# A 256 MB quadrant swap by DMA on one core: every half row on the sync queue, and SBUF copies of 2 to 6 KB issued from the scalar queue

## The chip, the cores and the metric

The kernel runs on one core of one Trainium2 chip. The metric is device time in microseconds (us). Two runs of the kernel before took 810.55 and 813.21 us, a median of 811.88 us. One further execution was taken with the hardware profiler; its own time is the span of 812.4 us, from the first to the last instruction.

A core has 16 DMA engines. They serve DMA queues that are filled by the sequencers of other engines: here SP (SyncE, the "sync queue") and ACT (ScalarE, the "scalar queue"). In the profile the two queues are q1 and q10. A DMA is cut into packets; here a packet is one contiguous run of bytes.

## The reference

```python
x = np.random.randn(8192, 8192).astype(np.float32)
return np.fft.ifftshift(x)
```

For even sizes this swaps the quadrants: `out[r, c] = x[(r + 4096) % 8192, (c + 4096) % 8192]`. Nothing is computed. 268.44 MB are read from HBM and 268.44 MB are written to HBM, in half rows of 4096 float32, which is 16 KB each.

## The kernel before, in words

Each DMA goes straight from HBM to HBM. It moves 256 half rows (4 MB): 16 half rows for each of the 16 DMA engines. The function `copy` (L26 to L32) writes the pattern as `[[C, 16], [step*C, 16], [1, 4096]]`. The first dimension is the DMA engine, so with `step = 16` engine e takes the rows e, e+16, e+32 and so on, and at any moment the 16 engines work on neighbouring rows.

There are 64 such DMAs. The loop at L36 to L39 issues them in pairs: SP copies the left half of 256 rows of the output (L38), ACT the right half of 256 rows that lie 512 rows away within the same group of 1024 rows (L39). So each queue has 32 DMAs.

What holds the issuing back is bookkeeping of the tile framework. It gives each DMA one of eight completion semaphores in turn, and a DMA waits until the one that had this semaphore before it is complete. The turn is the order that the framework's scheduler gives to the program, and not that of the text. In the kernel before SP and ACT alternate in that order, so each queue has four DMAs in flight, eight in all. No DMA depends on another one's data.

Of the kernel before, what the change touches and what calls it, by code (L numbers as in the profile page):

```python
# [1 line left out]

# [4 lines left out]


ENGINES = 16


@with_exitstack
def kernel(
    ctx: ExitStack,
    tc: tile.TileContext,
    x: bass.AP,
    out: bass.AP,
):
    nc = tc.nc
    R, C = x.shape  # L20
    hr = R // 2
    hc = C // 2
    per = 16
    rows = ENGINES * per

    def copy(queue, row, h, step):  # L26

        dims = [[C, ENGINES], [step * C, per], [1, hc]]
        queue.dma_start(
            out=bass.AP(out.tensor, out.offset + row * C + h, dims),  # L30
            in_=bass.AP(x.tensor, x.offset + (row + hr) % R * C + hc - h, dims),
        )  # L32

    for first in range(0, R, 4 * rows):  # L36
        for n in range(4):
            copy(nc.sync, first + n * rows, 0, ENGINES)  # L38
            copy(nc.scalar, first + (n + 2) % 4 * rows, hc, ENGINES)  # L39


# [1 line left out]
_INS = ['x']  # L43
_OUTS = [((8192, 8192), 'float32')]


def kernel(**inputs):
    import numpy as _np
    import concourse.bacc as _bacc
    import concourse.tile as _tile  # L50
    from concourse import mybir as _mybir
    from concourse.bass_utils import run_bass_kernel_spmd as _run

    nc = _bacc.Bacc("TRN2", target_bir_lowering=False, num_devices=1)  # L54
    arrays, args = {}, []
    for name in _INS:
        a = _np.ascontiguousarray(inputs[name])
        if a.dtype.kind in "iu":
            a = a.astype(_np.int64)
        arrays[f"in_{name}_dram"] = a  # L60
        args.append(nc.dram_tensor(f"in_{name}_dram", a.shape, _mybir.dt.from_np(a.dtype), kind="ExternalInput").ap())
    for i, (shape, dtype) in enumerate(_OUTS):
        dt = _mybir.dt.from_np(_np.dtype(dtype))
        args.append(nc.dram_tensor(f"out_{i}_dram", shape, dt, kind="ExternalOutput").ap())
    with _tile.TileContext(nc) as tc:
        kernel(tc, *args)
    r = _run(nc, [arrays], core_ids=[0])
    got = tuple(r.results[0][f"out_{i}_dram"] for i in range(len(_OUTS)))
    return got[0]
```

## Time and profile before

| what | value | where it stands |
|---|---|---|
| median of two runs | 811.88 us (810.55 and 813.21) | the times |
| profiled execution, own time = span | 812.4 us | the profile's page |
| HBM read and written | 268.44 MB and 268.44 MB, 661 GB/s together | the page, part 3 |
| DMAs on SP's and on ACT's queue | 32 and 32, of 4096 KB each | the page, part 6 |
| packets in all | 17408, of which 1024 under 512 B (16 for each of the 64 DMAs) | the page, part 2 |
| time from issue to landing, median | 101.0 us | the page, part 6 |

The compute engines do nothing here, apart from four small memsets of POOL at the start. So the chain of waits on the page has nothing to say, and the profile is read from its DMA rows: the busy share of the 16 DMA engines and the GB/s that they moved, in 40 slices of the span or in stretches that one chooses. "GB/s" counts each byte once, though it is read from HBM and written to HBM: 330 GB/s moved is 660 GB/s at the HBM.

### The profile page before, as it was taken

How to read it: one execution, taken by the hardware profiler on the slowest of the kernel's cores; microseconds unless marked ns; L12 is line 12 of the kernel's file. 1: busy time of each engine (PE TensorE's matmuls, PEld its weight loads, DVE VectorE, ACT ScalarE, POOL GpSimd, SP SyncE). 2: the span in 40 equal slices, each digit the busy share in tenths (PEclk: the TensorE clock that was granted, in tenths of full speed). 3: DMA queues.
4: the chain of work that ended last, by engine and by line, in shares of the span. 5: the costliest groups of instructions: out<-in, count | busy, mean ns of one | idle time of the engine just before them, and what ended most of it. 6: DMA issues, size and time to landing. Idle time of an engine off the chain costs nothing. (4 is left out here: it accounts for less than half of the span.)

```text
span 812.4 us, 109 instructions
## 1 busy us (share of the span) xinstructions
POOL 0.2 (0%) x4
## 2 busy tenths in 40 slices
POOL 0000000000000000000000000000000000000000
DMA  9999999999999999999999999999999999999998
GB/s 307 331 331 336 335 331 331 335 325 337 334 332 336 331 333 332 334 339 332 332 334 331 329 331 334 332 328 333 330 334 335 334 328 333 332 331 330 338 331 280
DMA packets 17408, 268.44 MB, mean 330 GB/s; under 512 B 1024, under 2 KB 1024, under 8 KB 1024
## 3 DMA queue, kind: packets, MB, share of 16 engines
q1 hardware_dynamic: 8704, 134.22, 49.7%
q10 hardware_dynamic: 8704, 134.22, 49.5%
HBM read 268.44 MB, written 268.44 MB: 661 GB/s over the span
## 5 line engine op out<-in xcount | busy, mean ns | idle before, releaser
L54 POOL MEMSET const-bfloat16-1.0<- 128x1 bf16 x1 | 0.1, 101 | 0.0
L54 POOL MEMSET const-uint8-127<- 128x1 uint8 x1 | 0.1, 101 | 0.0
L54 POOL MEMSET const-float32-0.0<- 128x1 f32 x1 | 0.1, 98 | 0.2 <-issue 0.2
L54 POOL MEMSET const-float32-1.0<- 128x1 f32 x1 | 0.1, 98 | 0.0
## 6 DMA issues: line engine op xcount, KB each, us to landing
out_dram<-in_x_dram SPq DMA_DIRECT2D x32, 4096.0 KB, 101.0
out_dram<-in_x_dram ACTq DMA_DIRECT2D x32, 4096.0 KB, 101.0
```

What stands on the lines that cost most here:

```text
L54: nc = _bacc.Bacc("TRN2", target_bir_lowering=False, num_devices=1)
```

## The change

All 64 copies of half rows are issued from SP (`nc.sync`, L42). Per 1024 rows of the output (an "eighth"), the order is now four DMAs of the left half and then four of the right half.

After each copy, except in the last eighth, ACT issues a `pace(n)` (L47 to L50): a DMA from one SBUF tile, `idle`, to a tile of a pool with six buffers, `into`. It moves `[128, 2, n]` float32 out of tiles of `[128, 2, 2064]`, so it consists of 256 runs of 4n bytes, 16 runs for each DMA engine. That is one run of SBUF bytes for each half row that the engine copies. `n` is 512, 768, 1024, 1280, 1536, 1024, 768 in the first seven eighths: runs of 2, 3, 4, 5, 6, 4 and 3 KB. There are 56 such DMAs, which move 56.6 MB. What they write is never read. VectorE fills `idle` with zeros once (L35), and the first `pace` waits for that.

In the sixth and seventh eighth `apart` is 16 and `by` is 1: engine e takes 16 rows that follow each other, and the 16 engines work 16 rows (512 KB) apart.

```diff
+    still = ctx.enter_context(tc.tile_pool(name="still", bufs=1))
+    paced = ctx.enter_context(tc.tile_pool(name="paced", bufs=6))
+    idle = still.tile([128, 2, longest + 16], f32)
+    nc.vector.memset(idle[:], 0.0)
-    def copy(queue, row, h, step):
+    def copy(row, h, apart, by):
-        dims = [[C, ENGINES], [step * C, per], [1, hc]]
-        queue.dma_start(
+        dims = [[apart * C, ENGINES], [by * C, per], [1, hc]]
...
+        nc.sync.dma_start(
...
+    def pace(n):
+        into = paced.tile([128, 2, longest + 16], f32, name="into")
+        nc.scalar.dma_start(out=into[:, :, :n], in_=idle[:, :, :n])
-    for first in range(0, R, 4 * rows):
-        for n in range(4):
-            copy(nc.sync, first + n * rows, 0, ENGINES)
-            copy(nc.scalar, first + (n + 2) % 4 * rows, hc, ENGINES)
+    part = 1024
+    for n, (piece, apart) in enumerate((
+        (512, 1), (768, 1), (1024, 1), (1280, 1), (1536, 1),
+        (1024, per), (768, per), (0, 1),
+    )):
+        for h in (0, hc):
+            for row in range(n * part, (n + 1) * part, rows):
+                copy(row, h, apart, ENGINES if apart == 1 else 1)
+                if piece:
+                    pace(piece)
```

The built program can be read before it runs. Call the copies C1 to C64 and the SBUF copies P1 to P56, each in the order of its queue. The scheduler put them, and so handed out the eight semaphores, in this order: C1, P1 to P34, C2, P35 to P56, C3 to C64. The waits that came of it are these (the letter after "waits" is the DMA that must be complete):

```
SP queue                       ACT queue
C1   waits for nothing         P1        waits for the memset of idle
C2   waits P27                 P2 to P6  wait for nothing
C3   waits P49                 P7        waits P1
C4   waits P50                 P8        waits P2 and C1
C5   waits P51                 P9 to P41 wait for the P six before (P9: P3)
...                            P42       waits P36 and C2
C10  waits P56                 P43 to P56 wait for the P six before
C11  waits C3
C12  waits C4, and so on to C64, which waits C56
```

## The prediction

> **What bounds the kernel now.** I read the page's DMA rows first, because no compute engine does anything.
>
> ```profile
> span 812.4 us, 109 instructions
> ...
> DMA  9999999999999999999999999999999999999998
> GB/s 307 331 331 336 335 331 331 335 325 337 334 332 336 331 333 332 334 339 332 332 334 331 329 331 334 332 328 333 330 334 335 334 328 333 332 331 330 338 331 280
> ...
> q1 hardware_dynamic: 8704, 134.22, 49.7%
> q10 hardware_dynamic: 8704, 134.22, 49.5%
> HBM read 268.44 MB, written 268.44 MB: 661 GB/s over the span
> ```
>
> All 16 DMA engines are busy in every slice, and the rate is flat at 332 GB/s. The two queues' packets fill 99.2% of the engines' time, so there is no gap to fill. Busy is not the same as at full speed, though. 99.2% of 16 x 812.4 us over 16384 data packets is 787 ns for a packet of 16 KB. In the trace's packet records the commonest duration is 611 ns (4,842 of the 16,384 packets), hardly any is shorter, and the others spread up to some 1,400 ns. I take 611 ns (26.8 GB/s, or 429 GB/s for 16 engines) as what an engine can do and the other 176 ns as waiting for the HBM, where all 16 engines read and write at once.
>
> Then I cut the span into stretches (us, length; then POOL, clock, DMA share, GB/s moved):
>
> ```profile
> 2.00:3.00 1.00, 0.00 (x0) 1.00 1.05 262
> 3.00:4.00 1.00, 0.00 (x0) 1.00 1.01 410
> 4.00:5.00 1.00, 0.00 (x0) 1.00 1.00 377
> 5.00:6.00 1.00, 0.00 (x0) 1.00 1.11 426
> 6.00:8.00 2.00, 0.00 (x0) 1.00 0.98 344
> 8.00:10.00 2.00, 0.00 (x0) 1.00 1.01 344
> 10.00:20.00 10.00, 0.00 (x0) 1.00 0.99 328
> ...
> 100.00:400.00 300.00, 0.00 (x0) 1.00 1.00 333
> ...
> 806.00:808.00 2.00, 0.00 (x0) 1.00 0.96 328
> ```
>
> From 3 to 6 us the kernel moved 404 GB/s, more than ever after. Up to 5 us only SP's queue had packets and the 16 engines ran in step. By 10 us both queues were at work, the engines had drifted apart, and the rate was that of the rest. The last row matters as well: in 806 to 808 us SP's queue had nearly run out (85% of the bytes were on ACT's queue by the packet records), the engines were out of step, and the rate was 328 GB/s.
>
> Last, the DMA queue's own waits, with what the sequencers waited for:
>
> ```profile
> SPq L29 <- DMA out_dram<-in_x_dram: 689.4, 28, 25.3
> SPq L65 <- DMA out_dram<-in_x_dram: 102.2, 2, 79.5
> ```
>
> The sequencers wait for landings for nearly all of the span, 25 us at most (two DMAs of 12.6 us). These waits cost nothing while eight DMAs are in flight. They cost all they last when what is awaited is not a copy of half rows, and that is where the change goes.
>
> **The change part by part.** The sum is made against the profiled execution, 812.4 us, 0.5 us above the median of the runs. At 332 GB/s a copy of 4.194 MB costs 12.63 us; 64 of them are 808.5 us, and 3.9 us are start and end (the first packet starts at 2.2 us).
>
> *The order.* The text reads as if each SBUF copy ran beside its half rows. The built program's waits say otherwise: C2 waits for P27, C3 for P49, C4 to C10 for P50 to P56. So the first 49 SBUF copies run with only C1 and C2 beside them, and the other 62 copies come after, with hardly any pacing. Where the HBM had work all the time, it now idles while SBUF copies to SBUF.
>
> *The first stretch, up to the landing of P49.* P1 to P48 are eight each of 512, 768, 1024, 1280, 1536 and 1024 columns, and P49 one of 768; a column is 1024 bytes (128 x 2 x 4). That is 51.1 MB, 3.19 MB for each engine. The trace of before has no SBUF copy. The floor is the 611 ns row, 26.8 GB/s: 119 us. The upper bound is the mean HBM packet, 787 ns for 16 KB: 154 us. I take the floor, because these packets don't touch the HBM, which is what makes the 787; I add 9 ns a packet, which is what a 4-byte semaphore packet takes in the records, for 49 x 16 packets: 7 us, together 126 us. Six SBUF copies are in flight, 7 us of work at the shortest length (1.2 us each), against 0.6 us to issue one and 1.4 us from issue to first packet, so latency doesn't show. The packets of C1 and C2 run on the same engines: 2 x 16 packets at the 656 to 689 ns of the first rounds, 21 us (ends 20 and 25). With the start at 2.2 us the stretch ends at 149 us, between 141 and 181. The memset of 4128 columns by VectorE isn't in the trace (the nearest row is POOL's 0.1 us for one column); C1's packets fill the engines until 12 us, so up to there it costs nothing, and beyond that it would cost what it takes longer. P8 waits for C1 and P42 for C2, which are done before.
>
> *Handing over.* C3 waits for P49, and from that landing to its first packet lie 0.6 us of issue and 1.4 us: 2 us, in which P50 to P55 go on.
>
> *P50 to P56.* 5.5 MB, 12.8 us of engine time at the floor, beside C3 to C10. Nothing of it shows if the half rows' packets only shorten their wait for the HBM (176 ns each, against 115 ns for a 3 KB run); all of it shows if not. I take the middle, 6 us.
>
> *The 62 other copies.* From C11 on each waits for the one eight before it, so eight are in flight as before, all on one queue. The row nearest to one queue with engines out of step is the 328 GB/s of 806 to 808 us; the row with one queue and engines in step is 404 GB/s. Here the engines come out of a mixture of SBUF and HBM packets, and nothing puts them in step again, so I take the steady 332: 62 x 12.63 = 783 us. The fast end is 62 x 10.4 = 644 us. For the slow end I take 3% more, the spread of the slices: 807 us. That left and right halves are 1024 rows in turn, and that C41 to C56 put the engines 512 KB apart, has no row of its own and stands within these ends.
>
> The sum is 149 + 2 + 6 + 783 + 2 (the end) = **942 us**, 130 more than before. Against 812.4: 147 us up to P49, 2 + 6 after it, less C1 and C2 that are done by then (25 us).
>
> Two places of the Trainium skill bear on the 62 copies. The Trainium skill's page HBM Reference, section Specifications (TRN2), gives about 716 GB/s for the HBM of a pair of cores; by it one core moves at most 358 GB/s from HBM to HBM, the 62 copies take at least 726 us and the whole at least 885. The trace does not agree in its first microseconds: 404 GB/s moved is 808 at the HBM, though for 3 us only. The Trainium skill's page DMA: Bandwidth & Descriptors, section Latency and other measured facts, has copies at a row pitch of 512 KiB at 207 GB/s where 214 was full rate; if that held for the 512 KB between engines in C41 to C56, it would add an estimated 7 us (16 x 12.63 x 0.034), and the sum would be 949. No trace here shows it.
>
> **The rivals.**
>
> *One queue keeps the engines in step* (ends on the other side). If it is the second queue that pulls the engines out of step, the 62 copies could go at the start's 404 GB/s: 149 + 2 + 6 + 644 + 2 = 803 us, no slower than before. For it speaks that the rate fell as ACT's packets came in. Against it speak 806 to 808 us, with one queue and 328 GB/s, and that packets of up to 1,188 ns come already in the fourth round of SP's packets. It decides from 11.6 us a copy (361 GB/s), which gives 878, below the lower end of the sum; it makes the change no slower by 2% (828 us) only from 10.8 us a copy (389 GB/s).
>
> *The pacing runs as the text reads*, one SBUF run for each half row, should the waits bind less than I read them. Then either the HBM stays the limit and the SBUF runs hide in its 176 ns (812 us and some more where runs are 5 and 6 KB: 611 + 191 and 611 + 229 ns are over 787, which is 15 and 53 ns on 2048 packets an eighth, over 16 engines 2 and 7 us, so 821), or the engines' time adds up (56.6 MB at 429 GB/s, 132 us, so 944). Against it stand the waits of the built program, which are counts that must be reached.
>
> *SBUF copies or one queue are slower than any row here.* At half the floor rate (13.4 GB/s an engine) P1 to P49 take 238 us and the whole is 1054. Nothing in the trace speaks for it but that it has no such row.
>
> **How the numbers follow.** I give the forecast 0.68, the rival with engines in step 0.15 (of it 0.02 faster and 0.04 within 2%), pacing as the text reads 0.05 (0.02 within 2%, the rest slower), and slower rows 0.12. The forecast's own range is 141 + 2 + 0 + 783 + 2 = 928 to 181 + 2 + 13 + 783 + 2 = 981. The range for 8 in 10 reaches down to 875, which takes in the weaker half of the first rival (one queue a little faster), and up to 985. Faster by over 2%: 0.02. Within 2%, about what a measurement of this kernel can tell from no change: 0.06. Slower by over 2%: 0.92.
>
> **What would show it.** In the profile after, the HBM moves its 661 GB/s only from some 150 us on. Before that ACT's queue carries 51 MB, the rate moved is near 429 GB/s, and only two of SP's copies have landed. SP's second issue comes near 70 us (P1 to P27 are 22.8 MB, 53 us, plus C1 and the start), its third near 149 us, and the longest wait of its queue is about 80 us. Afterwards the rate is 332 GB/s with packets of about 787 ns. I am wrong if the third copy is issued much before 140 us, if the last 600 us run far from 332 GB/s, or if SBUF packets of 2 to 6 KB take much more than 80 to 240 ns.

## The result, and the profile after

The changed kernel took 943.71 us (median of two runs, 940.75 and 946.67) against 811.88 us: 1.163 times as long, with a 95% interval of 1.153 to 1.173. Its profiled execution has a span of 938.6 us.

The DMA rows of the page after:

```profile
span 938.6 us, 168 instructions
...
DMA  9999999999999999999999999999999999999998
GB/s 322 409 416 402 423 417 404 377 376 334 333 330 330 335 331 337 335 326 334 338 335 330 336 336 334 332 337 335 334 337 336 333 333 338 333 332 332 332 336 294
...
q1 hardware_dynamic: 17408, 268.44, 84.6%
q10 hardware_dynamic: 15232, 56.63, 15.0%
HBM read 268.44 MB, written 268.44 MB: 572 GB/s over the span
```

The DMA engines are as busy as before, in every slice. They also move more: 346 GB/s on average. Neither line shows the loss. The last line does: the HBM went from 661 to 572 GB/s, which is the same bytes over a longer span. The row of GB/s says where. In the second to seventh slice (each is 23.5 us) the engines move above 400 GB/s, which HBM traffic never did for long before, and from the tenth slice up to the last but one it is at 326 to 338, as before.

The waits of SP's queue (us in total, times, longest):

```profile
SPq L42 <- DMA into<-idle: 205.5, 9, 78.2
SPq L87 <- DMA out_dram<-in_x_dram: 68.1, 4, 31.2
```

Nine times SP's queue waited not for a copy of half rows but for an SBUF copy, 205.5 us in all and 78.2 us the longest. Those are the waits of C2 to C10. The order of issue shows two of them (start, length, then engine, line and how many without a gap in between):

```profile
59.73 21.62 ACTq L50 DMA_DIRECT2D into<-idle  x6
71.55 0.59 SPq L42 DMA_DIRECT2D out_dram<-in_x_dram  x1
```

```profile
140.83 12.07 ACTq L50 DMA_DIRECT2D into<-idle  x6
150.34 9.96 SPq L42 DMA_DIRECT2D out_dram<-in_x_dram  x4
```

SP's second copy was issued at 71.55 us and the third at 150.34 us, half a microsecond after P49 had landed (149.8 us by the sixteenth of its semaphore packets). Cut at these points (us, length; VectorE, POOL, clock, DMA share, GB/s moved):

```profile
2.00:16.00 14.00, 3.16 (x1) 0.00 (x0) 1.00 0.98 324
16.00:71.00 55.00, 0.00 (x0) 0.00 (x0) 1.00 1.03 412
71.00:92.00 21.00, 0.00 (x0) 0.00 (x0) 1.00 1.01 399
92.00:150.00 58.00, 0.00 (x0) 0.00 (x0) 1.00 1.02 419
150.00:161.00 11.00, 0.00 (x0) 0.00 (x0) 1.00 1.03 394
161.00:212.00 51.00, 0.00 (x0) 0.00 (x0) 1.00 1.00 378
212.00:930.00 718.00, 0.00 (x0) 0.00 (x0) 1.00 1.00 334
```

In the second and the fourth stretch, 113 us together, the packet records hold not one packet of 16 KB: all of it is SBUF to SBUF, and the HBM idles. The first stretch holds C1, the third C2. From 212 us on it is the kernel before on one queue, at 334 GB/s.

The HBM idles longer than these two stretches, because the packets of C2 and C3 start late: C2's first one at 76.68 us, 5.1 us after its issue, and C3's at 155.50 us, 5.2 us after. By the packet records no half row is under way from 16.1 to 76.7 us and from 90.5 to 155.5 us, which is 125.6 us together. The span is 126.2 us longer than that of the kernel before, so this is all but the whole loss.

### The profile page after: what moved, and what is told of

Read it like the earlier page. It is cut to its first block, busy times and chain, and to the rows that moved or that the text cites. A ratio compares the mean times of both kernels' runs of the same rounds, so it can differ in the third digit from the quotient of the medians.

```text
span 938.6 us, 168 instructions
## 1 busy us (share of the span) xinstructions
DVE 3.5 (0%) x1; POOL 0.2 (0%) x4
## 5 line engine op out<-in xcount | busy, mean ns | idle before, releaser
L35 DVE MEMSET idle<- 128x4128 f32 x1 | 3.5, 3498 | 1.7 <-PEq L76 1.7
```

The source lines that it names most:

```text
L35: nc.vector.memset(idle[:], 0.0)
```

## The experiments

The theory, called the order theory below: the 132 us (943.71 less 811.88) were lost because the built order puts 49 SBUF copies ahead of 62 copies of half rows, so the HBM idles while they run. It has a rival with the same sum for this kernel: SBUF bytes take the DMA engines' time wherever they stand, and 56.6 MB at 410 to 429 GB/s are 132 to 138 us. A second rival puts the loss on the one queue and the row patterns. The first three runs tell these apart. The last three measure what an SBUF run costs. The first three kernels share runs of the kernel before with a median of 810.97 us. The last three were timed later, together with runs of the kernel before that took 823.41 us; why those took 1.5% more is not known. Each ratio is to the runs of its own group.

**The copies alone, on one queue.**

```diff
-    nc.vector.memset(idle[:], 0.0)
+    nc.vector.memset(idle[:, :, :16], 0.0)
...
                 copy(row, h, apart, ENGINES if apart == 1 else 1)
-                if piece:
-                    pace(piece)
```

> The changed kernel without its 56 SBUF copies (so it leaves out only work that the output does not need): 64 copies of half rows on SP's queue in the same order and with the same row patterns, eight in flight. Order theory (the loss is the time in which SBUF copies run with at most two copies of half rows beside them): 64 x 12.63 us and 4 us at the ends, 812 us, within 1% of before. Rival, one queue or the row patterns cost or gain something by themselves: the time differs from 812 by what they do, above 828 if they cost; if one queue kept the engines in step (404 GB/s) about 670.

Measured: 814.85 us against 810.97, a ratio of 1.005 (1.002 to 1.008). The page of that run:

```profile
GB/s 302 327 321 334 328 324 332 331 322 335 321 339 335 334 337 337 333 327 335 340 330 334 332 332 328 329 335 339 331 330 331 334 337 334 340 335 331 331 330 294
...
q1 hardware_dynamic: 17408, 268.44, 99.2%
HBM read 268.44 MB, written 268.44 MB: 660 GB/s over the span
```

The one queue and the patterns cost half a per cent, 4 of the 132 us. One queue does not hold the 404 GB/s of the start either: the rate is flat at 332 from the second slice on. The Trainium skill's page DMA: Bandwidth & Descriptors, section Issuing engines are not separate DMA queues, says that a second issuing engine only saves the time of issuing; this run agrees, with 1.005 for one queue in place of two. The eighths with the engines 512 KB apart stand out in nothing: 100.9 and 100.0 us against 100.4 to 101.9 for the second to fifth. The forecast took 3% for them from the Trainium skill's page DMA: Bandwidth & Descriptors, section Latency and other measured facts, where the pitch of 512 KiB lies between the rows of partitions. Between these two patterns the 3% did not appear. In the other eighths, though, the rows of one engine lie 512 KB apart, so no run here shows a copy without that pitch.

**The same 120 DMAs, in the order of the text.** Each DMA gets an edge of issue order to the one before it, which orders the scheduler and adds no wait:

```diff
+    def behind(one, other):
...
+            tc.add_manual_dep(
+                one.ins,
+                other.ins.name,
+                mybir.DependencyInfo(
+                    mybir.DependencyClass.NoSync, mybir.DependencyReason.DATA
+                ),
+                reason="order",
+            )
+        return one
...
-                copy(row, h, apart, ENGINES if apart == 1 else 1)
+                last = behind(copy(row, h, apart, ENGINES if apart == 1 else 1), last)
                 if piece:
-                    pace(piece)
+                    last = behind(pace(piece), last)
```

> The same DMAs as in the changed kernel, all 120 of them, in the order of the text: each copy and each SBUF copy gets an edge of issue order to the one before it, so SP and ACT take turns and each DMA waits only for the one of its own queue four before. Order theory: the HBM has work all the time, SBUF runs hide for the most part in the wait for the HBM (beside P53 to P56, of 3 KB, a copy took 12.97 us and not 12.63, which hides five sixths of their 2.0 us), and where a half row and its run together exceed 787 ns (5 and 6 KB) they add some: 820 to 850 us. Rival, the SBUF bytes cost the DMA engines' time wherever they stand (56.6 MB at 410 to 429 GB/s, 132 to 138 us): 940 to 950 us, the same as the changed kernel.

Measured: 826.44 us, a ratio of 1.019 (1.015 to 1.024). The same bytes in another order cost 15 us and not 132. So the rival of the bytes falls, and the order, with the waits that come of it, is the cause. SP's queue now waits for copies of half rows, and for SBUF copies only twice:

```profile
SPq L42 <- DMA out_dram<-in_x_dram: 657.6, 55, 13.2
...
SPq L42 <- DMA into<-idle: 14.7, 2, 7.5
```

Its packet records have no gap of over 0.5 us without a half row under way. The run's stretches are cut at the eighths (half rows' starts in the packet records):

```profile
2.00:105.00 103.00, 3.16 (x1) 0.00 (x0) 1.00 1.00 365
105.00:206.00 101.00, 0.00 (x0) 0.00 (x0) 1.00 1.01 393
206.00:306.00 100.00, 0.00 (x0) 0.00 (x0) 1.00 1.01 416
306.00:409.00 103.00, 0.00 (x0) 0.00 (x0) 1.00 1.01 427
409.00:516.00 107.00, 0.00 (x0) 0.00 (x0) 1.00 1.01 430
516.00:617.00 101.00, 0.00 (x0) 0.00 (x0) 1.00 1.01 417
617.00:718.00 101.00, 0.00 (x0) 0.00 (x0) 1.00 1.01 397
718.00:820.00 102.00, 0.00 (x0) 0.00 (x0) 1.00 0.98 333
```

The GB/s rise and fall with the length of the SBUF runs, while an eighth stays at 101 us. By the packet records:

| SBUF run | its packet, ns | half row's packet, ns | both, ns | an eighth, us |
|---|---|---|---|---|
| none (before) | | 787 | 787 | 100.2 to 102.8 |
| 2 KB | 84 | 726 | 810 | 102.3 |
| 3 KB | 121 | 677 | 798 | 101.2 |
| 4 KB | 159 | 634 | 793 | 100.3 |
| 5 KB | 196 | 615 | 811 | 102.7 |
| 6 KB | 234 | 611 | 845 | 106.9 |

The five rows with SBUF runs are the first five eighths of this run. Each SBUF run takes its time out of the half row's wait: the sum stays at 787 to 811 ns until the half row is down to 611 ns and nothing is left to take from. Then the engine is the limit. What the table does not show is a gain. With fewer engines at the HBM at a time each half row is faster (634 ns beside 4 KB runs), but the HBM delivers no more than before: the third eighth takes 100.3 us beside 4 KB runs and took 100.8 without.

**All on one queue.**

```diff
-        nc.scalar.dma_start(out=into[:, :, :n], in_=idle[:, :, :n])
+        nc.sync.dma_start(out=into[:, :, :n], in_=idle[:, :, :n])
```

> The SBUF copies issued from SP as well, so that all 120 DMAs stand in the order of the text on one queue: on each DMA engine 16 half rows, then 16 SBUF runs, and so on. Order theory: while one engine is at its SBUF runs the others have more of the HBM, so it is much as with turns between two queues, 820 to 860 us, provided that the engines are out of step; if they reach their SBUF runs together, the HBM idles for the 1.3 to 3.8 us of each SBUF copy and it is near 812 + 132 = 944. Rival, the bytes cost the engines' time wherever they stand: 940 to 950.

Measured: 830.99 us, a ratio of 1.024 (1.020 to 1.029). The queue keeps the order of the text by itself, and blocks of 16 half rows and 16 SBUF runs hide nearly as well as single ones in turn: the first seven eighths take 101.8, 102.2, 101.2, 102.6, 107.0, 101.1 and 101.2 us, as in the run before. The last one, which has no SBUF copies, took 109.6 us and not 103.4. There the engines finished far apart: from 820 to 830 us they were busy for 17% of the time, against 64% in the last ten microseconds of the interleaved run (812 to 822). Why they drifted that far stays open.

**Half the length, order as the scheduler has it.**

```diff
-        (512, 1), (768, 1), (1024, 1), (1280, 1), (1536, 1),
-        (1024, per), (768, per), (0, 1),
+        (256, 1), (384, 1), (512, 1), (640, 1), (768, 1),
+        (512, per), (384, per), (0, 1),
```

> The changed kernel with all SBUF runs half as long (1 to 3 KB), the order left to the scheduler as before. In the built program the split is the same or a little sharper: C1, then P1 to P56, then C2 to C64, with C2 waiting for P49 and C3 to C9 for P50 to P56. Order theory: the first stretch costs what its bytes cost, P1 to P49 are now 25.6 MB, 62 us at 410 GB/s, so 2 us of start, 12 of C1, 62 of SBUF copies, 2 of handing over, 63 x 12.63 = 796, some 3 for P50 to P56 and 2 at the end: about 878 us, half of the loss. Rival, a stall at the start that goes by the number of SBUF copies and their semaphores and not by their bytes: near 940, as with the full lengths.

Measured: 895.43 us against 823.41, a ratio of 1.090 (1.086 to 1.095): 72 us lost where 66 were expected. SP's queue waited for SBUF copies again, 79.9 us at the longest, and C2 was issued at 81.4 us:

```profile
SPq L42 <- DMA into<-idle: 113.9, 7, 79.9
```

```profile
16.00:81.00 65.00, 0.00 (x0) 0.00 (x0) 1.00 1.04 389
```

No half row is under way from 16.0 to 86.8 us by the packet records, 70.8 of the 72 us. The loss goes by the bytes and not by the number of SBUF copies, so a stall that goes by their number falls. Of the 6 us more than expected some 3 lie in this stretch: runs of 1 KB take 46 ns (22 GB/s for an engine, against 26 for 4 KB), so it moves 389 GB/s and not 410. Another 3 lie in the handing over: C2's first packet started 5.4 us after its issue, where 2 were expected.

**4 KB everywhere, in turns.** The edges of issue order as above, and one length:

```diff
-        (512, 1), (768, 1), (1024, 1), (1280, 1), (1536, 1),
-        (1024, per), (768, per), (0, 1),
+        (1024, 1), (1024, 1), (1024, 1), (1024, 1), (1024, 1),
+        (1024, 1), (1024, 1), (1024, 1),
```

> All DMAs in turns, as in the interleaved run, with SBUF runs of 4 KB (1024 columns) in all eight eighths and the row pattern of the first five everywhere; 64 SBUF copies. Slack theory (a DMA engine has 176 ns of waiting in each half row's 787 ns; an SBUF run that fits in costs nothing, and the HBM's 332 GB/s stay the limit): a run takes 159 ns, so 812 us, within 1% of before; the eighth with 4 KB runs took 100.3 us there against 101.1 of before, which would make 806 at best. Rival, fewer engines at the HBM at a time make it faster (the durations of the half rows fell to 634 ns beside 4 KB runs): well under 800.

Measured: 833.42 us against 823.41, a ratio of 1.012 (1.009 to 1.014). The rival, a gain, falls. The slack theory (that a run shorter than the 176 ns of wait costs nothing) is off by 1%: 67 MB of SBUF copies cost 10 us. In the profiled execution (837.25 us, the slowest of the six) the half rows take 656 ns beside the 159, which is 815 ns, where the interleaved run, of the faster group, had 793. The first seven eighths took 102.3 to 103.9 us and the last one 107.1, so part of the loss lies at the end. It may be that an SBUF run that fits the mean wait does not fit every single one. That is not shown: the 4 KB eighths of the interleaved run lost nothing (100.3 and 101.3 us, against 100.8 and 101.3 before), and there is no profile of the kernel before from this later group.

**8 KB everywhere, in turns** (2048 in place of 1024 in the edit above).

> The same turns with SBUF runs of 8 KB (2048 columns) everywhere, longer than any slack. Slack theory: the engine is the limit, 611 + 309 ns (84 ns for 2 KB and 37.5 ns more for each KB) for each of 1024 half rows, 942 us, perhaps 1% less as with 6 KB runs (106.9 us an eighth against 108.2 by this sum); the half rows take 611 ns. Rival, SBUF runs hide whatever their length as long as they stand beside half rows: 812 us.

Measured: 943.79 us against 823.41, a ratio of 1.146 (1.144 to 1.149), as the engine's time gives it. The page:

```profile
GB/s 355 431 429 431 429 432 428 432 431 428 431 429 431 430 433 430 430 430 431 429 431 431 432 429 431 430 431 429 433 430 429 431 429 430 431 433 429 431 430 397
DMA packets 34816, 402.66 MB, mean 428 GB/s; under 512 B 2048, under 2 KB 2048, under 8 KB 2048
...
HBM read 268.44 MB, written 268.44 MB: 570 GB/s over the span
```

428 GB/s, flat: the 26.8 GB/s of an engine, 16 times. 99% of the half rows' packets take 611 ns, and the HBM has 570 GB/s to do. This is what the rival of the bytes looks like where it is true. Its HBM line (570) is the same as that of the changed kernel (572), and only the row of slices tells the two apart: flat here, two levels there.

## Why the prediction was right

*The order.* The forecast took C2 to wait for P27 and C3 for P49, from the built program. Issues at 71.55 and 150.34 us answer to the 70 and 149 us that it named, and the 125.6 us without a half row are shown. That this order is the cause, and not the bytes, was only argued in the forecast; the interleaved run shows it.

*The first stretch.* Forecast 149 us, measured 149.8. The packets of P1 to P49 sum to 126.2 us per engine (16 for each DMA, at 85, 124, 161, 203 and 236 ns for 2 to 6 KB), where the floor and 9 ns a packet gave 126. The row chosen, 611 ns for 16 KB, was right because SBUF packets do run at that rate; the bound of 787 ns a 16 KB would have been 28 us too much. The memset took 3.5 us and lay beside C1. The packets of C1 and C2 took 12.8 and 10.4 us per engine, 23.1 and not 21: those of C1 took 797 ns on average, while the 656 to 689 ns that the forecast put in were those of the third round alone. The parts measured (2.2 + 126.2 + 23.1) are 1.7 us over the 149.8, because the records of one engine's packets overlap a little: the DMA share is 1.03 and 1.02 in the two stretches of SBUF copies.

*Handing over and P50 to P56.* C3's issue to C10's landing (258.4 us) is 108.1 us for eight copies, 13.5 us each, 7 us more than at 12.63. The forecast had 2 + 6, but the parts are otherwise. C3's first packet started 5.7 us after P49's landing, because it came 5.2 us after the issue and not 1.4. The 1.4 us are those of C1, whose packets met idle engines. The kernel before already had a row for a second queue: ACT's first DMA was issued at 0.73 us, and its first packet started at 5.06 us. So this term was 4 us too small, and that of P50 to P56 too large by more than that: beside C3 to C10 they show next to nothing. That the two cancel is luck.

*The 62 other copies.* Forecast 783 us; from C3's first packet to the end of C64 it was 781.9 us, with what was left of P50 to P56 in it. From P49's landing it was 787.6 us (forecast 791). The steady 332 GB/s was the row to take. The slow end of 807 us that the forecast worked out for these copies went into neither bound; with it the forecast's own range would have reached 1005 us and not 981.

*The rival with engines in step.* In the start of the changed kernel one queue was alone up to 9.6 us. The rate was 404 GB/s from 3 to 6 us, as in the kernel before, and 300 from 6 to 9 us. So the fall needs no second queue, which the kernel before could not show, because its second queue came in at 5 us. The copies alone confirm it over a whole run. The 404 is a little high in both: a stretch counts a packet where it starts, and the DMA share of these 3 us is 1.04 before and 1.07 after.

*Pacing as the text reads.* The built waits excluded it for this kernel. The forecast gave two ends for it, 821 us hidden and 944 added up. Made to happen, it took 826 us, near the hidden end.

The sum was made against the profiled execution, whose span is 938.6 us after, so 942 is 3 us too much. It was also what the wrong mechanism would have given (944). The agreement of the total is therefore no evidence for the order; the waits, the slices and the interleaved run are.

## What to carry to other kernels

Where a scheduler gives out a few completion semaphores in turn, a DMA can wait for another with which it shares no data; read the built order and its waits, not the text, before you cost DMAs that should run beside each other, and fix the order with edges of issue order where it matters. "DMA 9 in every slice" says that the engines have packets, not that the bottleneck has work: put the HBM's GB/s next to it. Where packets wait for the HBM, other DMA work can use up most of that wait for little (4 KB beside every 16 KB cost 1.2% here), but it does not make the HBM faster, and pacing the engines gained nothing at any length tried here.

## What the runs showed of the hardware

A DMA engine's SBUF to SBUF packets have little fixed cost at 2 to 6 KB: 84, 121, 159, 196 and 234 ns beside half rows, 37.5 ns for each KB and 9 ns more. With 8 KB runs in turn all 16 engines held 428 GB/s for 940 us.

The HBM's rate for these half rows, 332 GB/s moved, did not depend on how many engines asked at a time: it was the same with the half rows at 787 ns each and at 634. The 404 GB/s of 3 to 6 us were gone after 6 us on one queue as on two. What keeps the HBM at 661 GB/s once the engines are out of step was not found.

A DMA's first packet started 1.4 to 1.5 us after its issue where it was the first of the kernel (0.73 to 2.2 us), and 4.2 to 5.4 us after where another queue's packets were on the engines: 0.73 to 5.06 us before, 71.55 to 76.68 and 150.34 to 155.50 us after, 81.41 to 86.79 us with half the length. What makes the difference was not found.
